# First products of an FFN: eight column tiles instead of four, the new four in seven block products

## The chip, the cores and the metric

The kernel runs on one core of a Trainium2 chip. The metric is the device time of one execution in microseconds (us). TensorE (PE) multiplies matrices into PSUM; VectorE (DVE) and ScalarE (ACT) work on tiles in SBUF and PSUM; GpSimd (POOL) does a little; SyncE (SP) issues the transfers from memory.

## The reference

Two layers (DEPTH = 2) of a post-norm encoder on 256 tokens of width 1024, all in float32:

```
for l in range(DEPTH):
    x = layer_norm(ALPHA * x + 0.5 * swiglu(x, ffn1_w_in[l], ffn1_w_out[l]), ...)
    x = layer_norm(ALPHA * x + hybrid_mixer(x, ...), ...)
    x = layer_norm(ALPHA * x + 0.5 * swiglu(x, ffn2_w_in[l], ffn2_w_out[l]), ...)

def swiglu(x, w_in, w_out):
    h = x @ w_in                               # 1024 -> 2 * 2816
    gate, up = h[..., :D_FF], h[..., D_FF:]
    return (silu(gate) * up) @ w_out           # 2816 -> 1024
```

The mixer (differential attention beside windowed attention) isn't touched by the change. There are four FFNs, two in each layer: (l, n) = (0, 0), (0, 2), (1, 0), (1, 2).

## The kernel before, in words

**Two halves of every number.** Most products are made in the type fp32r. Each operand is split in a high half (a cast to fp32r on ScalarE) and a low half (the value less the high half, on VectorE), and a product is made of three matmuls: high by high, high by low, low by high. `Weights._make` loads a row of weights (128 x 1024, 512 KB, issued on SP) into a `raw` buffer (there are 5), casts it to `wh` (L118) and subtracts it to `wl` (L119); there are 9 buffers of each. The window LOOK keeps at most nine of these slots ahead of use. The two instructions of a split have a priority lowered by LATER.

**An FFN.** The 2816 hidden columns are 22 column tiles of 128, each with a gate and an up half, and the 1024 inputs are 8 row tiles. Tokens come in two halves t of 128.

- `first`: the first four column tiles (NB = 4) with the tokens stationary: for each t and each of the 8 weight rows, three matmuls for gate and three for up, 512 columns wide. Then SiLU and a product (`gvb`, L390), and `first_t` transposes the result on TensorE (L397) and splits it into `gs` (L401, L402). In the first FFN both t run over the rows in one pass, and the DMA of the inputs has only begun; in the others t = 0 has its own pass, in which x of t = 1 is transposed by `to_xt`, and t = 1 has a second pass over the same 8 rows, which frees their slots.
- `col`: the other 18 column tiles with the weights stationary: for gate and up each 8 wide matmuls (both halves of all 256 tokens, 512 columns, L419) and 8 narrow ones (the weights' low half by the tokens' high half, 256 columns, L424). One tile alone comes first (column tile 4), then `first_t` of t = 1, then another one alone (column tile 5), then couples of two. With `flip` the narrow ones come first. After each tile comes an epilogue: a copy (L434), an addition (L435), SiLU (L436), the product (L438) and the split (L441, L442).
- the out phase: the second product of the FFN. Ten of the 22 row tiles are taken in five pairs (`STR`, indices of pairs of column tiles), the others one by one (`step`). `pair` computes the product of a 2 x 2 block matrix (two token halves, two row tiles, two column halves) by seven block products instead of eight. For that `_make_pair` builds four sums of weight blocks on VectorE (L86 to L89), and splits three 1024-wide tiles and one 512-wide (L72, L73); a pair takes 3 `raw` buffers, 4 slots of `wh` and `wl`, and one `tmp` tile. `sums` builds four sums of blocks of the activations (L457 to L462).
- then the tail of single steps, and the layer norm.

**What sets the order.** TensorE's order is the program's. The other engines' instructions are ordered by a scheduler at compile time by priority; each engine then runs its own list in order. Tiles of one tag share their buffers: `g` has 11, `tmp` 7, `x` 5, PSUM 8 (the pool `ps`, a bank each). The rotary table is computed on VectorE in the first FFN behind the first couple of column tiles.

Of the kernel before, what the change touches and what calls it, by code (L numbers as in the profile page):

```python
# [9 lines left out]
F32 = mybir.dt.float32  # L10
F32R = mybir.dt.float32r
# [8 lines left out]
P = 128  # L20
SEQ = 256
# [33 lines left out]
0; P sq 1 1; V 1; O 0 2; T sq 1; O 0 2; B 0 0; S s 1; B 0 1; Y 1; W 0 0; W 0 1; S s 1; O 1 1; O 0 1; O 1 1; O 0  # L55
3; B 1 0; B 1 1; W 1 0; W 1 1; O 1 2; Z; O 1 4
"""


class Weights:  # L60
# [15 lines left out]
    def _make_pair(self, i):  # L76


        nc, dv = self.nc, self.nc.vector
        r0, r1, ta = (self.pool.tile([P, 1024], F32, tag="raw", name=f"raw{i}{c}", bufs=5) for c in "abt")  # L80
        for r, src in zip((r0, r1), self.srcs[i][1:]):
            nc.sync.dma_start(r, src)
        t4 = self.tmp.tile([P, 512], F32, tag="tmp", name=f"t4_{i}")
        a, b = slice(0, 512), slice(512, 1024)
        with self.tc.high_priority(-LATER):
            dv.tensor_tensor(ta[:, a], r0[:, b], r0[:, a], ALU.subtract)  # L86
            dv.tensor_tensor(ta[:, b], r0[:, b], r1[:, b], ALU.add)
# [11 lines left out]
    def _make(self, i):  # L99
        nc = self.nc  # L100
        if self.srcs[i][0] == "S":
            return self._make_pair(i)
        raw = self.pool.tile([P, 1024], F32, tag="raw", name=f"raw{i}", bufs=5)
        wh = self.pool.tile([P, 1024], F32R, tag="wh", name=f"wh{i}", bufs=9)
        wl = self.pool.tile([P, 1024], F32R, tag="wl", name=f"wl{i}", bufs=9)

        n = 512 if i < 3 else 1024
        src = self.srcs[i]

        rows = src if isinstance(src, tuple) else (src,)  # L110
        for c in range(0, 1024, n):
            s = slice(c, c + n)
            for q, r in enumerate(rows):
                h = P // len(rows)

                (nc.sync if i or c else nc.scalar).dma_start(raw[q * h : (q + 1) * h, s], r[:, s])
            with self.tc.high_priority(0 if i < 3 else -LATER):
                nc.scalar.copy(wh[:, s], raw[:, s])  # L118
                nc.vector.tensor_tensor(wl[:, s], raw[:, s], wh[:, s].bitcast(F32), ALU.subtract)  # L119
        self.made.append((wh, wl))  # L120
# [15 lines left out]
def encoder_kernel(  # L136
# [44 lines left out]
    def out_rows(w):  # L181
        row = lambda k: w[k * P : (k + 1) * P, :]
        rows = [row(k) if u == "o" else ("S", row(2 * k), row(2 * k + 1)) for u, k in plan]
        return rows + [row(k) for k in tail]

    srcs = []
    for l in range(DEPTH):
        srcs += [f1_b[l, k] for k in range(KT)]
        srcs += [f1_in[l, j, s] for j in range(JT - NB) for s in range(2)]
        srcs += out_rows(f1_out[l])  # L190
        for c in range(3):
            srcs += [m_in[l, c, q] for q in range(4)]
# [6 lines left out]
        srcs += [f2_b[l, k] for k in range(KT)]  # L199
        srcs += [f2_in[l, j, s] for j in range(JT - NB) for s in range(2)]  # L200
        srcs += out_rows(f2_out[l])
    W = Weights(tc, wp, tp, srcs)
    wi = 0
# [113 lines left out]
        nc.sync.dma_start(bt, ln_b[l, n].partition_broadcast(P))  # L317
        return gt, bt

    def to_xt(src, t, nm, hs=(0, 1), gain=None):  # L320

        with tc.high_priority():
            for h in hs:
                tr = ps.tile([P, 4, P], F32, tag="b", name=f"tr_{nm}{t}{h}")
                for i in range(4):
                    c = (4 * h + i) * P
                    nc.tensor.transpose(tr[:, i, :], src[:, c : c + P], ident)
                dh = xx[:, 4 * h : 4 * h + 4, 0, t, :]
                dl = xx[:, 4 * h : 4 * h + 4, 1, t, :]
                if gain is None:  # L330
                    nc.scalar.copy(dh, tr)
                    dv.tensor_tensor(dl, tr, dh.bitcast(F32), ALU.subtract)
                else:
                    nc.scalar.mul(dh, tr, gain)
                    dv.scalar_tensor_tensor(dl, tr, gain, dh.bitcast(F32), ALU.mult, ALU.subtract)
# [25 lines left out]
    def ffn(l, n, last=False):  # L361
        nonlocal wi
        nm = f"{l}{n}"
        gs = [gp.tile([P, 2, 2, SEQ], F32R, tag="g", name=f"g_{nm}_{q}") for q in range(JT // 2)]

        def first(ts, mid=None):

# [23 lines left out]
                out.append(gv)  # L391
            return out

        def first_t(gv, t):
            tr = ps.tile([P, 4, P], F32, tag="b", name=f"trg_{nm}{t}")
            for i in range(4):
                nc.tensor.transpose(tr[:, i, :], gv[:, i * P : (i + 1) * P], ident)  # L397
            for q in range(2):
                a = slice(t * P, (t + 1) * P)
                dh = gs[q][:, :, 0, a]  # L400
                nc.scalar.copy(dh, tr[:, 2 * q : 2 * q + 2, :])  # L401
                dv.tensor_tensor(gs[q][:, :, 1, a], tr[:, 2 * q : 2 * q + 2, :], dh.bitcast(F32), ALU.subtract)  # L402

        def col(*js, flip=False):

            nonlocal wi
            ts = []
            for j in js:

                hs = [ps.tile([P, 2, SEQ], F32, tag="b", name=f"h{'gu'[s]}_{nm}_{j}") for s in range(2)]  # L410
                tl = tp.tile([P, 2, SEQ], F32, tag="tl", name=f"tl_{nm}_{j}", bufs=2)
                ws = [W.get(wi), W.get(wi + 1)]
                wi += 2
                ts.append((j, hs, tl, ws))

            def wide(hs, ws, s):
                for k in range(KT):

                    mm(hs[s], ws[s][0][:, k * P : (k + 1) * P], xx[:, k], start=(k == 0 and not flip),  # L419
                       stop=(k == KT - 1 and flip), skip_group_check=flip)  # L420

            def narrow(hs, ws, s):
                for k in range(KT):
                    mm(hs[s][:, 1, :], ws[s][1][:, k * P : (k + 1) * P], xx[:, k, 0], start=(k == 0 and flip),  # L424
                       stop=(k == KT - 1 and not flip), skip_group_check=flip)

            one, two = (narrow, wide) if flip else (wide, narrow)
            for j, hs, tl, ws in ts:
                for s in range(2):
                    one(hs, ws, s)  # L430
            for j, hs, tl, ws in ts:
                for s in range(2):
                    two(hs, ws, s)
                    nc.scalar.copy(tl[:, s], hs[s][:, 1, :])  # L434
                    dv.tensor_tensor(tl[:, s], hs[s][:, 0, :], tl[:, s], ALU.add)  # L435
# [3 lines left out]
                q, jj = divmod(j, 2)  # L439
                n = P if q in STR and jj == 0 else SEQ  # L440
                nc.scalar.copy(gs[q][:, jj, 0, 0:n], gv[:, 0:n])  # L441
                dv.tensor_tensor(gs[q][:, jj, 1, 0:n], gv[:, 0:n], gs[q][:, jj, 0, 0:n].bitcast(F32), ALU.subtract)  # L442
                if q in STR and jj:
                    sums(q, ts[0][2][:, 1], gv)

        sm = {}

# [18 lines left out]
        if first_x:  # L466
            g0, g1 = first((0, 1))
        else:
            (g0,) = first((0,), lambda: to_xt(x[1], 1, f"x{nm}"))
            (g1,) = first((1,))  # L470
        wi += KT
        if not first_x:
# [89 lines left out]
        todo += [(i, [c]) for c in fin for i in range(TAIL - SPLIT, TAIL)]  # L562
        for n_, (i, cs) in enumerate(todo):
            if n_ == len(todo) - TCUT and not last:
                to_xt(x[0], 0, f"y{nm}")
# [18 lines left out]
    def mixer(l):  # L584
# [263 lines left out]
        for tok in ORDER.split(";"):  # L848
# [37 lines left out]
            elif op == "X":  # L886
                to_xt(x[1], 1, f"m{l}")
            elif op == "Z":
                to_xt(x[0], 0, f"z{l}")
            elif op == "S":  # L890
                do_s(*ar)
            elif op == "A":
# [89 lines left out]
```

## Time and profile before

| | |
|---|---|
| three runs, us | 931.63, 931.92, 932.51 (median 931.92) |
| the profiled execution | 931.88 us, span 930.1 us, granted clock 0.997 |
| busy us: PE, DVE, ACT | 922.0, 789.5, 569.1 |
| transfers | 176.29 MB, mean 190 GB/s |

The span is from the first to the last recorded instruction. In the profile "PE" is the matmuls, "PEld" the loading of stationary operands, "xN" the number of instructions. In lists of instructions in order of time the columns are start (us), duration (us), engine, line, operation, output and inputs, shapes, and in brackets how long the engine sat idle before it and what ended that. The stages by TensorE in order: first FFN 4.8 to 186 us, mixer to 283, second FFN to 464, third FFN to 645, mixer to 743, fourth FFN to the end.

### The profile page before, as it was taken

Reading aid. Unit: us, or ns where it says so; the run is one execution under the profiler, and the core shown is the slowest. Engines: PE = TensorE matmul, PEld = TensorE weight load, DVE = VectorE, ACT = ScalarE, POOL = GpSimd, SP = SyncE. Lnnn points to the kernel's source line nnn. Section 1 sums busy time; section 2 is a strip of 40 time slices with the busy share of each in tenths; the row PEclk is TensorE's granted clock in tenths of the full one; section 3 lists DMA queues with packets and bytes.
Section 4 is the critical chain, followed back from the end, with each engine's and each line's share of the span. In section 5 each row is a group of like instructions: output and inputs, shape, how many; then the busy total and the mean of one; then the engine's idle time right before and its main releaser. Section 6 shows DMA issues by size and latency. Waiting matters only on the chain.

```text
span 930.1 us, 13767 instructions
## 1 busy us (share of the span) xinstructions
PE 922.0 (99%) x4970; PEld 788.2 (85%) x4970; DVE 789.5 (85%) x1344; ACT 569.1 (61%) x970; POOL 17.0 (2%) x27
## 2 busy tenths in 40 slices
PE   9999999999999999999999999999999999999996
PEld 7888888888888888888888888888888889888885
DVE  7898899998987678899986888999988976888896
ACT  5768656546865666656546666663478656666650
POOL 0000000000000000000000000000000000000000
PEclk9999999999999999999999999999999999999998
DMA  9986546675426755547675665575844365665551
GB/s 315 310 271 202 159 145 218 226 248 152 125 90 206 245 181 181 161 154 218 224 254 191 187 194 162 158 254 175 275 112 137 107 228 188 193 190 159 159 180 46
DMA packets 51379, 176.29 MB, mean 190 GB/s; under 512 B 6512, under 2 KB 8304, under 8 KB 51312
## 3 DMA queue, kind: packets, MB, share of 16 engines
q1 hardware_dynamic: 51024, 175.03, 58.7%
q8 instruction: 39, 0.64, 0.3%
q10 hardware_dynamic: 288, 0.39, 0.1%
q14 instruction: 28, 0.23, 0.1%
HBM read 174.35 MB, written 1.05 MB: 189 GB/s over the span
## 4 chain that ended last, share of the span: by engine, by line
PE 99%; DVE 1%; issue 0%; DVEq 0%
PE hg L419 14%; PE hu L419 14%; PE acc L503 14%; PE hb L381 9%; PE hu L424 7%; PE hg L424 7%; PE pp L527 6%; PE ao L840 5%; PE acc L527 4%; PE os L776 1%; PE pj_sq L619 1%; PE pj_sq L617 1%; PE pj_dv L617 1%; PE pj_sq L618 1%; PE pj_dq L617 1%; PE pj_dv L619 1%
## 5 line engine op out<-in xcount | busy, mean ns | idle before, releaser
L119 DVE TENSOR_TENSOR wl<-raw,wh 128x1024 fp32r<-128x1024 f32 (+1 forms) x279 | 336.1, 1210 | 73.7 <-PE hg L424 28.8
L118 ACT CAST wh<-raw 128x1024 fp32r<-128x1024 f32 (+1 forms) x279 | 290.6, 1047 | 117.4 <-PE acc L503 29.3
L419 PE MATMUL hg<-xx,wh 128*128 128x512 f32 x576 | 143.2, 391 | 0.0
L419 PE MATMUL hu<-xx,wh 128*128 128x512 f32 x576 | 142.3, 389 | 0.0
L419 PEld LDWEIGHTS hu<-xx,wh 128*128 128x128 f32 x576 | 108.1, 188 | 22.5
L419 PEld LDWEIGHTS hg<-xx,wh 128*128 128x128 f32 x576 | 106.6, 188 | 21.2
L503 PE MATMUL acc<-wh,g 128*128 128x512 f32 (+1 forms) x390 | 109.0, 387 | 0.0
L503 PEld LDWEIGHTS acc<-wh,g 128*128 128x128 f32 x390 | 72.9, 188 | 14.7
L424 PE MATMUL hg<-xx,wl 128*128 128x256 f32 x576 | 81.0, 283 | 0.0
L424 PE MATMUL hu<-xx,wl 128*128 128x256 f32 x576 | 80.9, 283 | 0.0
L424 PEld LDWEIGHTS hg<-xx,wl 128*128 128x128 f32 x576 | 75.4, 192 | 1.6
L424 PEld LDWEIGHTS hu<-xx,wl 128*128 128x128 f32 x576 | 74.3, 192 | 0.0
L381 PE MATMUL hb<-wh,xx 128*128 128x512 f32 x256 | 70.3, 395 | 0.0
L503 PE MATMUL acc<-wl,g 128*128 128x512 f32 (+1 forms) x195 | 61.6, 386 | 0.0
L381 PEld LDWEIGHTS hb<-wh,xx 128*128 128x128 f32 x256 | 48.3, 190 | 10.5 <-ACT wh L118 0.6
L434 ACT COPY tl<-hg 128x256 f32<-128x256 f32 x72 | 26.8, 372 | 32.0 <-PE hg L419 28.1
L503 PEld LDWEIGHTS acc<-wl,g 128*128 128x128 f32 x195 | 36.6, 188 | 7.3
L434 ACT COPY tl<-hu 128x256 f32<-128x256 f32 x72 | 26.8, 372 | 20.2 <-PE hu L424 17.1
L381 PE MATMUL hb<-wl,xx 128*128 128x512 f32 x128 | 38.9, 391 | 0.0
L840 PE MATMUL ao<-wh,xx 128*128 128x512 f32 x128 | 37.0, 398 | 0.0
L441 ACT CAST g<-tl 128x128 fp32r<-128x128 f32 (+1 forms) x72 | 27.1, 376 | 15.9 <-DVE tl L438 14.0
L436 ACT ACTIVATE tl<-tl 128x256 f32<-128x256 f32 x72 | 30.2, 419 | 6.5 <-DVE tl L435 5.6
(972 smaller groups left out, 1477.4 us busy)
## 6 DMA issues: line engine op xcount, KB each, us to landing
raw<-in_f_in_dram SPq DMA_DIRECT2D x144, 512.0 KB, 4.4
raw<-in_f_out_dram SPq DMA_DIRECT2D x48, 512.0 KB, 4.1
raw<-in_m_in_dram SPq DMA_DIRECT2D x36, 512.0 KB, 4.7
raw<-in_f_b_dram SPq DMA_DIRECT2D x29, 512.0 KB, 4.3
raw<-in_m_out_dram SPq DMA_DIRECT2D x8, 512.0 KB, 4.7
raw<-in_m_out_dram SPq DMA_DIRECT2D x16, 256.0 KB, 4.4
lng<-in_ln_g_dram SPq DMA_DIRECT2D x6, 512.0 KB, 4.9
lnb<-in_ln_b_dram SPq DMA_DIRECT2D x6, 512.0 KB, 6.0
```

The lines of the kernel that those rows point to most:

```text
L118: nc.scalar.copy(wh[:, s], raw[:, s])
L119: nc.vector.tensor_tensor(wl[:, s], raw[:, s], wh[:, s].bitcast(F32), ALU.subtract)
L381: mm(hb[s], xx[:, k, g, t, :], ww[:, 512 * s : 512 * s + 512], start=(k == 0 and e == 0), stop=(k == KT - 1 and e == 2))
L419: mm(hs[s], ws[s][0][:, k * P : (k + 1) * P], xx[:, k], start=(k == 0 and not flip), stop=(k == KT - 1 and flip), skip_group_check=flip)
L424: mm(hs[s][:, 1, :], ws[s][1][:, k * P : (k + 1) * P], xx[:, k, 0], start=(k == 0 and flip), stop=(k == KT - 1 and not flip), skip_group_c ...
L434: nc.scalar.copy(tl[:, s], hs[s][:, 1, :])
L436: nc.scalar.activation(tl[:, 0], tl[:, 0], AF.Silu)
L441: nc.scalar.copy(gs[q][:, jj, 0, 0:n], gv[:, 0:n])
L503: mm(a, g, ww[:, s], start=(k == ka and e == 0), stop=(k == kb and e == 2))
L527: mm(o, g, ww, start=(own and first and e == 0), stop=(own and final and e == 2))
L617: mm(o, xx[:, k, 0, t, :], wh[:, s], start=(k == 0), stop=False)
L840: mm(acc[t][h], xx[:, k, g, t, :], ww[:, s], start=(k == 0 and e == 0), stop=(k == KT - 1 and e == 2))
```

## The change

The tokens-stationary part now takes eight column tiles (NB = 8): the first four (NF = 4) as before, the next four in `group`. There the product of the tokens (two halves t by two row tiles of a pair k) and the weights (two row tiles by gate and up, 512 columns each) is made by seven block products of three matmuls each, for four pairs of row tiles, accumulated in seven PSUM banks: 84 matmuls of 512 columns. `_make_pair` makes the weights' sums as in the out phase, for four pairs in a row. `x_sums` makes four sums of blocks of x and their splits, from an unsplit copy of the transposed x (`xkeep`), which `to_xt` now stores by one more ScalarE copy per half, at a priority lowered by KEEP; in the first FFN it comes by two DMAs of 512 KB, issued on SP. The group's results are put together by nine VectorE instructions and three on ScalarE; two more calls of `first_t` transpose them after column tile 9.

The order in an FFN is now: `first` (rows 0 to 7), `first_t` (in the first FFN later), `x_sums`, column tile 8, `first_t`, `group`, column tile 9, `first_t` twice, the couples 10 and 11 to 20 and 21. The weights are fetched in that order: 8 rows, 2 rows of column tile 8, 4 pairs, the other columns' rows. The weights of the eight tiles lie together in memory, so that the 8 rows and the pairs' rows are read in runs of 2 KB per partition instead of 4 KB. STR goes from (3, 4, 5, 6, 7) to (5, 6, 7, 8, 9). The `gs` tiles are allocated one by one when first written.

```diff
-NB = 4
+NF = 4
+KEEP = 20
+NB = 8
-STR = (3, 4, 5, 6, 7)
+STR = (5, 6, 7, 8, 9)
...
+    def in_rows(b, w):
+        blk = lambda g, k: b[k].rearrange("p (s g c) -> p g s c", s=2, g=NB // NF)[:, g]
+        cols = [w[j, s] for j in range(JT - NB) for s in range(2)]
+        return [blk(0, k) for k in range(KT)] + cols[:2] + [("S", blk(1, 2 * k), blk(1, 2 * k + 1)) for k in range(KT // 2)] + cols[2:]
...
-        srcs += [f1_b[l, k] for k in range(KT)]
-        srcs += [f1_in[l, j, s] for j in range(JT - NB) for s in range(2)]
+        srcs += in_rows(f1_b[l], f1_in[l])
...
                     nc.scalar.copy(dh, tr)
                     dv.tensor_tensor(dl, tr, dh.bitcast(F32), ALU.subtract)
+                    if keep:
+                        with tc.high_priority(-KEEP):
+                            nc.scalar.copy(xkeep[t][:, 4 * h : 4 * h + 4, :], tr)
...
+        def split(src, nm_):
+            s = gp.tile([P, 2, 4, P], F32R, tag="g", name=f"sx_{nm}_{nm_}")
+            nc.scalar.copy(s[:, 0], src)
+            dv.tensor_tensor(s[:, 1], src, s[:, 0].bitcast(F32), ALU.subtract)
+            return s
+
+        def x_sums():
+            v = [xkeep[t].rearrange("p (k e) c -> p k e c", e=2) for t in range(2)]
+            a11, a12, a21, a22 = v[0][:, :, 0], v[0][:, :, 1], v[1][:, :, 0], v[1][:, :, 1]
...
+            dv.tensor_tensor(s1, a21, a22, ALU.subtract)
+            dv.tensor_tensor(s2, a11, s1, ALU.subtract)
+            dv.tensor_tensor(s3, a21, a11, ALU.subtract)
+            dv.tensor_tensor(s4, a12, s2, ALU.subtract)
...
+        def group(xs):
+            b = {c: ps.tile([P, 512], F32, tag="b", name=f"pg_{nm}_{c}") for c in range(1, 8)}
+            for k in range(KT // 2):
+                b11, b21, b22, t4, t1, t2, t3 = W.get(wi)
+                wi += 1
...
+                what = {1: (blk(0, 0), b11), 2: (blk(1, 0), b21), 3: (s4, b22), 4: (blk(1, 1), t4),
+                        5: (s1, t1), 6: (s2, t2), 7: (s3, t3)}
+                for c in (2, 3, 5, 7, 1, 6, 4) if k < KT // 2 - 1 else (1, 2, 6, 7, 5, 3, 4):
+                    (ah, al), (bh, bl) = what[c]
+                    for e, (a_, w_) in enumerate(((ah, bh), (ah, bl), (al, bh))):
+                        mm(b[c], a_, w_, start=(k == 0 and e == 0), stop=(k == KT // 2 - 1 and e == 2))
+            f = lambda c: tp.tile([P, 512], F32, tag="tmp", name=f"gr_{nm}_{c}")
+            add = lambda o, p, v: dv.tensor_tensor(o, p, v, ALU.add)
...
+            nc.scalar.copy(v, b[1])
+            add(g0, b[2], v)
+            nc.scalar.activation(g0, g0, AF.Silu)
+            add(v, b[6], v)
+            add(w, b[7], v)
+            add(v, b[5], v)
+            add(u1, b[5], w)
+            add(v, b[3], v)
+            dv.tensor_tensor(v, g0, v, ALU.mult)
+            add(w, b[4], w)
+            nc.scalar.activation(w, w, AF.Silu)
+            dv.tensor_tensor(w, w, u1, ALU.mult)
+            return v, w
...
+        if first_x:
+            for t in range(2):
+                xkeep[t] = gp.tile([P, KT, P], F32, tag="g", name=f"xf_{nm}{t}")
+                nc.sync.dma_start(xkeep[t], x_tr[:, t])
+        else:
             first_t(g0, 0)
+        xs = x_sums()
         col(NB)
         if first_x:
             first_t(g0, 0)
         first_t(g1, 1)
+        ga, gb_ = group(xs)
         for j in (NB + 1, *range(NB + 2, JT, 2)):
             col(*((j,) if j == NB + 1 else (j, j + 1)), flip=(j % 4 == 0 or j == NB + 1))
+            if j == NB + 1:
+                first_t(ga, 0, NF // 2)
+                first_t(gb_, 1, NF // 2)
```

More of the change, by code (lines that the diff above doesn't have):

```diff
@@ L57, with _cols @@
 """
+def _cols(t, like):
+    return t if len(like.shape) == 2 else t.rearrange("p (s c) -> p s c", s=like.shape[1])
 class Weights:
@@ L198, in encoder_kernel @@
                  for n in range(KT // 2)]
[L199 to L200 removed]
+        srcs += in_rows(f2_b[l], f2_in[l])
         srcs += out_rows(f2_out[l])
@@ L363, in ffn, with g_tiles @@
         nm = f"{l}{n}"
-        gs = [gp.tile([P, 2, 2, SEQ], F32R, tag="g", name=f"g_{nm}_{q}") for q in range(JT // 2)]
+        gs = {}
+        def g_tiles(*qs):
+            for q in qs:
+                gs[q] = gp.tile([P, 2, 2, SEQ], F32R, tag="g", name=f"g_{nm}_{q}")
         def first(ts, mid=None):
@@ L392, in first, with first_t @@
             return out
-        def first_t(gv, t):
-            tr = ps.tile([P, 4, P], F32, tag="b", name=f"trg_{nm}{t}")
+        def first_t(gv, t, q0=0):
+            if not t:
+                g_tiles(q0, q0 + 1)
+            tr = ps.tile([P, 4, P], F32, tag="b", name=f"trg_{nm}{t}{q0}")
             for i in range(4):
@@ L468, in ffn @@
         else:
-            (g0,) = first((0,), lambda: to_xt(x[1], 1, f"x{nm}"))
+            (g0,) = first((0,), lambda: to_xt(x[1], 1, f"x{nm}", keep=True))
             (g1,) = first((1,))
         wi += KT
-        if not first_x:
+        if first_x:
+            for t in range(2):
+                xkeep[t] = gp.tile([P, KT, P], F32, tag="g", name=f"xf_{nm}{t}")
+                nc.sync.dma_start(xkeep[t], x_tr[:, t])
+        else:
             first_t(g0, 0)
+        xs = x_sums()
         col(NB)
```

34 lines of the change are left out of this document (27 added, 7 removed).

## The prediction

> **What bounds the kernel now.** I read the page's busy shares first, then the chain that ended last, then stretches of the span by engine, and last the instructions in order of time around the edit.
>
> ```profile
> span 930.1 us, 13767 instructions
> PE 922.0 (99%) x4970; PEld 788.2 (85%) x4970; DVE 789.5 (85%) x1344; ACT 569.1 (61%) x970; POOL 17.0 (2%) x27
> ...
> PE 99%; DVE 1%; issue 0%; DVEq 0%
> ```
>
> TensorE is busy 922.0 of 930.1 us and carries 99% of the chain: today nothing else ends last. VectorE follows with 789.5, so it has about 140 us to spare in the whole program. What matters is where that spare time lies:
>
> ```profile
> 0.00:24.00 24.00, 23.23 (x90) 17.25 (x91) 17.07 (x24) 13.64 (x16) 1.63 (x11) 1.00 0.90 314
> 27.60:33.10 5.50, 5.50 (x34) 4.88 (x33) 5.50 (x6) 3.86 (x6) 0.00 (x0) 1.00 0.97 316
> 27.60:165.80 138.20, 138.20 (x750) 120.44 (x749) 122.00 (x226) 95.98 (x154) 0.00 (x0) 1.00 0.67 216
> 283.30:306.40 23.10, 23.10 (x110) 19.23 (x109) 17.12 (x22) 11.78 (x13) 1.00 (x1) 1.00 0.67 220
> 312.00:406.80 94.80, 94.80 (x550) 84.10 (x548) 75.35 (x139) 60.42 (x109) 0.00 (x0) 1.00 0.55 169
> 406.80:444.20 37.40, 37.40 (x167) 30.97 (x166) 34.35 (x39) 23.32 (x27) 0.00 (x0) 1.00 0.67 210
> ```
>
> A row gives the stretch and its length, then busy us of PE, PEld, DVE (VectorE), ACT (ScalarE) and POOL, the granted clock, the DMA share and GB/s. In an FFN's column tiles it has 19.5 us of 94.8 free, spread out, while the out phase with its block products keeps it at 34.35 of 37.40. Around the place of the edit in the very first FFN (27.6 to 33.1) it is full already.
>
> **TensorE's part of the change.** Four column tiles leave the old scheme, seven block products for four pairs of row tiles come in.
>
> ```profile
> 54.48 1.84 PE hg L419 x8
> 76.69 1.84 PE hg L419 x8
> 135.18 2.72 PE pp L527 x12
> 305.81 0.60 PE L397 MATMUL trg<-ident,gvb 128*128 128x128 f32 x4
> 306.17 2.09 PE L419 MATMUL hg<-xx,wh 128*128 128x512 f32 x8
> ```
>
> Two flips apart, four column tiles take 76.69 - 54.48 = 22.21 us. Twelve block-product matmuls take 2.72, 0.227 each, and the group has 4 x 7 x 3 = 84: 19.04, or 4.76 a pair. Four transposes take 306.17 - 305.81 = 0.36; eight more cost 0.72. TensorE saves 22.21 - 19.04 - 0.72 = 2.45 us an FFN, **9.8 us in four**, if it never waits.
>
> **VectorE's part.** What counts is the distance between starts, since an instruction's reported end overlaps the next start:
>
> ```profile
> 425.88 1.22 DVE L73 TENSOR_TENSOR wl139t<-raw139t,wh139t 128x1024 fp32r<-128x1024 f32 x1
> 427.02 1.22 DVE L73 TENSOR_TENSOR wl139a<-raw139a,wh139a 128x1024 fp32r<-128x1024 f32 x1
> 428.16 0.69 DVE L86 TENSOR_TENSOR raw140t<-raw140a 128x512 f32<-128x512 f32 x1
> 428.76 0.69 DVE L73 TENSOR_TENSOR wl139f<-t,wh139f 128x512 fp32r<-128x512 f32 x1
> 429.36 0.69 DVE L87 TENSOR_TENSOR raw140t<-raw140a,raw140b 128x512 f32<-128x512 f32 x1
> ...
> 349.60 0.42 DVE L435 TENSOR_TENSOR tl<-hg,tl 128x256 f32<-128x256 f32 x1
> 349.93 0.42 DVE L435 TENSOR_TENSOR tl<-hu,tl 128x256 f32<-128x256 f32 x1
> ```
>
> 1024 columns: 1.14; 512: 0.60; 256: 0.33. Removed per FFN: eight row splits (9.1) and four column epilogues of four 256-wide instructions (5.3), 14.4 in all. Added: four weight pairs, each four block sums, three 1024 splits and one 512 split (5 x 0.60 + 3 x 1.14 = 6.42), 25.7; x_sums, four sums and four splits, 4.8; the group's epilogue, nine instructions, 5.4; four 256 splits, 1.3. Together 37.2. Net **+22.8 an FFN**, 91 in four: 789.5 becomes about 881 of a TensorE-only span of some 920. It fits on average. It does not fit locally: a pair costs VectorE 6.42 and TensorE 4.76, and four stand in a row.
>
> [...] If each instruction held the engine for its reported 1.22 or 0.69, a pair would cost 7.1 and the sum below would end near 957. The starts 0.60 apart at durations of 0.69 disagree, so the pitch stands and that end gets no chance below.
>
> **Where the group waits.** In the last pair the products run b11 first, so it needs nearly the whole pair made (all but the 512 split t4). I compare when TensorE is due at pair 4 with when VectorE can have made it, counting its work from when it is next free. Second FFN:
>
> ```profile
> 289.36 1.41 DVE L355 SCALAR_TENSOR_TENSOR x<-x,rs,lnb 128x512 f32<-128x512 f32 x2
> 292.56 1.29 DVE L332 TENSOR_TENSOR xx<-tr_x,xx 128x512 fp32r<-128x512 f32 x2 [1.79 <-ACT xx L331]
> 295.53 0.69 DVE L390 TENSOR_TENSOR gvb<-sgb,hb 128x512 f32<-128x512 f32 x1 [1.68 <-ACT sgb L388]
> 297.58 8.03 DVE L119 TENSOR_TENSOR wl<-raw,wh 128x1024 fp32r<-128x1024 f32 x6 [1.35 <-ACT wh L118]
> ```
>
> Layer norm ends at 290.8. The three gaps behind it (1.79, 1.68, 1.35) and everything from 297.6 are open to new work; the wait at 297.58 is for slots of the row weights, which block sums and x_sums don't need. Due: column tile 306.17 + 5.55 (a quarter of 22.21), 0.36 of transposes, three pairs of 4.76: 326.4. Needed before it: three pairs 19.3, the fourth without t4 5.8, x_sums 4.8, one column row 1.1, xx 1.2, two gvb 1.2, first_t 1.3, the column's epilogue 1.3: 36.0. Without a gap that ends at 326.8, and at the out phase's 92% (34.35 of 37.40) at 329.9. TensorE waits 0.4 to 3.5; I take 2.0. Net -0.45. The last FFN repeats this stage 459.4 later: -0.45.
>
> Third FFN:
>
> ```profile
> 471.07 2.35 DVE L119 TENSOR_TENSOR wl<-raw,wh 128x1024 fp32r<-128x1024 f32 x2
> 473.44 1.29 DVE L332 TENSOR_TENSOR xx<-tr_x,xx 128x512 fp32r<-128x512 f32 x2
> ...
> 487.30 1.85 PE hg L419 x8
> ...
> 306.42 1.85 PE hg L419 x8
> ```
>
> TensorE is 180.9 later than in the second (487.30 against 306.42), so due at 507.3; VectorE is free only at 473.4, ready at 509.4 to 512.5. Wait 2.1 to 5.2, taken 3.7: net +1.25.
>
> First FFN. The weights come at the DMA's pace: by 24.0 us 24 x 314 GB/s = 7.5 MB have landed, of which x and the eight rows are 5.2, so four more 0.5 MB blocks: two column rows and pair 1. VectorE has caught up by then:
>
> ```profile
> 18.53 6.35 DVE L119 TENSOR_TENSOR wl<-raw,wh 128x1024 fp32r<-128x1024 f32 x5
> 26.23 1.23 DVE L119 TENSOR_TENSOR wl<-raw,wh 128x1024 fp32r<-128x1024 f32 x1 [1.35 <-PE hb L381]
> 32.95 1.04 PE L397 MATMUL trg<-ident,gvb 128*128 128x128 f32 x8
> 33.74 1.20 PE L424 MATMUL hg<-xx,wl 128*128 128x256 f32 x8
> ```
>
> From 24.0: pair 1 without its first sum 5.8, pairs 2 and 3 12.8, the fourth 5.8, x_sums 4.8 (its 1 MB of x, queued behind pair 1 on SP, lands some 3 us later and the pair's own work fills that), gvb 1.2, first_t 1.3, the epilogue 1.3: 33.0, so 57.0, or 59.9 at 92%. The group starts at 33.74, pair 4 is due at 48.0. **Wait 9.0 to 11.9, taken 10.0**: net +7.55. Behind the group stands the rotary table, which needs VectorE where there is no spare time now:
>
> ```profile
> L275 DVE SCALAR_TENSOR_TENSOR rt<-rt 128x64 f32<-128x64 f32 x14 | 3.1, 220 | 0.0
> ```
>
> With as many smaller ones beside these 3.1 us, an estimate of 6 us; tiles 12 and 13 start with their low halves and would wait for them 0 to 4. I take 2.
>
> Costed at nothing: ScalarE (at 61%; it makes one copy for each split of VectorE's, so its extra is below 91 us and its spare 361; if it fell behind, the splits behind each copy would wait in order); seven of eight PSUM banks, since column tile 8's two are read out within some 2 us and the product that takes the last comes 2 us into the group (0 to 1 us); low halves for column tile 9, made while pair 4 runs; the keep copies; the moved STR, whose same sums come four tiles later and are still ready before the out phase. After the group VectorE has per two tiles 4 x 1.14 + 8 x 0.33 and the sums of a couple, under 2 (an estimate from the widths above), 9 of 11.1 us, so the lead it lost is regained in the six following couples.
>
> **Sum**: 7.55 + 2 - 0.45 + 1.25 - 0.45 = +9.9 on the profiled execution's 931.88 (span 930.1 and 1.8 around it; the median of the runs is 931.92): **941.8**. With all waits at their low ends (9.0, 0, 0.4, 2.1, 0.4) it is +2.1, 934.0; at their high ends (11.9, 4, 3.5, 5.2, 3.5) +18.3, 950.2. That is the likeliest case's own range.
>
> **Rivals.**
> - VectorE keeps up and TensorE stays the bound: -9.8, 922.1. For it: the waits of FFNs two to four are small sums of large numbers, and earlier spare time (17.12 of 23.10 busy) could take more. Against: the first FFN's 9 us rests on landing times. It decides if pair 1 is made in the first FFN before 20 us and the others start ahead of 290. [...]
> - Half and half: the first wait is about 5 and the others vanish; gains and waits cancel, 930 to 934.
> - The lost lead isn't regained. If VectorE runs no stretch better than 92%, the first FFN's 122.0 + 22.8 us take 157 instead of 138, and the second's 17.12 + 75.35 + 34.35 + 22.8 take 163 where its three stretches have 155: +19 and three times +7, 972. I count half of it, 952. For it: the out phase is at that share; against: columns have slack after the group.
> - First-product rows now come in runs of 2 KB, not 4. Against 409 GB/s with mostly long runs stood 270 with short ones:
>
> ```profile
> 4.00:8.00 4.00, 4.00 (x13) 2.85 (x12) 3.21 (x7) 1.60 (x3) 0.00 (x0) 1.00 0.94 270
> 12.00:16.00 4.00, 4.00 (x19) 3.34 (x18) 3.04 (x4) 2.64 (x3) 0.00 (x0) 1.00 1.04 409
> ```
>
>   At 270, five rows (2.6 MB) and pair 1 (1 MB) land 4.6 us later and the first FFN's chain with them: 946. Against: the early stretch also has the smaller x blocks. [...]
>
> **Chances.** Forecast 0.55, keeps up 0.17, cancels 0.10, lead lost 0.10, short runs 0.08. Faster by over 0.2% (1.9 us, about what a measurement can tell here) 0.20, within 0.10, slower 0.70. Range: 926 (the better half of the keeps-up case left out) to 953.
>
> **What would show it.** Right: gaps of PE before the block products of pairs 2 to 4, released by VectorE's splits wl of those pairs, some 10 us in the first FFN and 0 to 5 in the others; VectorE at 95% or more there; its total near 880; TensorE's busy time about 10 us less. Wrong: no PE gap in the first group, or waits that end on a DMA, on PSUM banks or on x_sums' own copies on ScalarE; or a PE pitch in the group other than 0.227.

## The result and the profile after

The changed kernel takes 954.62 us (median; 953.34 to 955.44) against 931.91: a ratio of 1.0243, 95% interval 1.0231 to 1.0256. It is slower by 22.7 us. The forecast was +9.9, and the time lies 1.6 us above the range's upper end of 953. Ratios here and below are against the kernel before, with the 95% interval in brackets. One of the ten executions of the kernel with single rows in all four FFNs, below, took 3301.84 us where the nine others took 933.45 to 933.88, and is left out of its ratio.

The page of the changed kernel, in the order in which that of the kernel before was read (span, busy shares, the chain by engine):

```profile
span 953.6 us, 13658 instructions
PE 925.7 (97%) x4826; PEld 778.4 (82%) x4826; DVE 870.6 (91%) x1460; ACT 596.3 (63%) x993; POOL 17.0 (2%) x27
...
PE 81%; DVE 13%; DMA 3%; ACT 1%; issue 1%; SPq 0%; DVEq 0%; ACTq 0%
```

TensorE issues 144 matmuls fewer, and yet its busy time is 925.7 where it was 922.0: a matmul of 512 columns is recorded with 0.63 us where the granted clock was 0.50 and with about 0.50 alone beside a wait (below), instead of 0.39 in the groups' undisturbed stretches. VectorE went from 789.5 to 870.6, and it now stands in the chain with 13%.

The share of the loss that each FFN has can be read from the first matmul of each out phase. The timeline of the changed kernel, and of the kernel before:

```profile
141.03 0.62 PE L596 MATMUL acc<-wh,g 128*128 128x512 f32 x2
422.70 0.61 PE L596 MATMUL acc<-wh,g 128*128 128x512 f32 x2
607.26 0.62 PE L596 MATMUL acc<-wh,g 128*128 128x512 f32 x2
889.90 0.62 PE L596 MATMUL acc<-wh,g 128*128 128x512 f32 x2
```

```profile
128.22 0.62 PE L503 MATMUL acc<-wh,g 128*128 128x512 f32 x2
406.67 0.62 PE L503 MATMUL acc<-wh,g 128*128 128x512 f32 x2
587.55 0.62 PE L503 MATMUL acc<-wh,g 128*128 128x512 f32 x2
866.03 0.62 PE L503 MATMUL acc<-wh,g 128*128 128x512 f32 x2
```

The lag is 12.8, 16.0, 19.7 and 23.9 us, so the four FFNs cost 12.8, 3.2, 3.7 and 4.2 us.

Inside an FFN there are two stops. The first is in the group. In the second FFN the group runs from its first block product to the low half that follows it:

```profile
325.06 0.48 PE L512 MATMUL pg<-wh93b,xx 128*128 128x512 f32 x1
...
341.27 0.49 PE L512 MATMUL pg<-wh96a,xx 128*128 128x512 f32 x1 [1.13 <-ACT wh96a L78]
342.94 0.50 PE L512 MATMUL pg<-wl96a,xx 128*128 128x512 f32 x1 [1.17 <-DVE wl96a L79]
...
347.62 0.52 PE L449 MATMUL hg<-xx,wl 128*128 128x256 f32 x3
```

It takes 22.56 us where 84 matmuls at 0.227 are 19.04. Of the excess of 3.52, 0.64 stands in pair 1 (5.40 us from start to start, in place of 4.76) and 2.88 at pair 4 (row 96). A bracket gives TensorE's idle time and its releaser; the two hold 2.30, and the rest is that a lone matmul is recorded with 0.49 where the next one otherwise starts after 0.227. The releasers are the cast and the split of one block of pair 4's weights. The cast had itself waited for VectorE: it starts at 340.18, after 0.74 us idle, when VectorE has made the block `raw96a` (second row below). VectorE at that time, without a gap:

```profile
338.19 1.22 DVE L79 TENSOR_TENSOR wl96b<-raw96b,wh96b 128x1024 fp32r<-128x1024 f32 x1
339.33 0.68 DVE L94 TENSOR_TENSOR raw96a<-raw96b,raw96t 128x512 f32<-128x512 f32 x1
339.93 1.22 DVE L79 TENSOR_TENSOR wl96t<-raw96t,wh96t 128x1024 fp32r<-128x1024 f32 x1
341.06 0.68 DVE L95 TENSOR_TENSOR t<-raw96b,raw96a 128x512 f32<-128x512 f32 x1
341.67 1.22 DVE L79 TENSOR_TENSOR wl96a<-raw96a,wh96a 128x1024 fp32r<-128x1024 f32 x1
```

The second stop comes behind column tile 9, where the group's results are transposed:

```profile
354.06 0.66 PE L422 MATMUL trg<-ident,gr_v 128*128 128x128 f32 x4 [0.71 <-DVE gr_v L524]
355.56 0.66 PE L422 MATMUL trg<-ident,gr_w 128*128 128x128 f32 x4 [0.84 <-DVE gr_w L527]
355.98 1.39 PE L444 MATMUL hg<-xx,wh 128*128 128x512 f32 x5
```

The eight transposes were to take 0.72. From the end of column tile 9 (347.62 + 5.58 = 353.20) to the next matmul it is 2.78, so 2.06 us are lost. VectorE is in the middle of the group's epilogue here, with splits of the next rows (L127) between its sums:

```profile
347.47 0.68 DVE L514 TENSOR_TENSOR gr_v<-pg,gr_v 128x512 f32<-128x512 f32 x1
348.07 1.21 DVE L127 TENSOR_TENSOR wl<-raw,wh 128x1024 fp32r<-128x1024 f32 x1
349.20 0.68 DVE L514 TENSOR_TENSOR gr_w<-pg,gr_v 128x512 f32<-128x512 f32 x1
...
354.82 0.69 DVE L527 TENSOR_TENSOR gr_w<-gr_w,gr_u 128x512 f32<-128x512 f32 x1 [0.47 <-ACT gr_w L526]
```

In the third FFN it is the same, with 0.89 us of VectorE's own wait for the cast of a row among it. In the first and the fourth FFN (1.57 us lost in each) TensorE waits for gr_w alone, 1.28 us by the bracket, and there VectorE is not busy. It stands idle before the last product of the epilogue, 1.92 and 1.47 us. In the first FFN:

```profile
72.19 0.37 ACT L459 COPY tl<-hu 128x256 f32<-128x256 f32 x1 [0.50 <-PE hu L444]
72.47 0.63 ACT L526 ACTIVATE gr_w<-gr_w 128x512 f32<-128x512 f32 x1
73.13 0.69 DVE L527 TENSOR_TENSOR gr_w<-gr_w,gr_u 128x512 f32<-128x512 f32 x1 [1.92 <-ACT gr_w L526]
```

VectorE had made the input of this SiLU by 70.27 (the sum starts at 69.59 and takes 0.68). But in ScalarE's own order the SiLU stands behind a copy of column tile 9 (L459), which can only come when TensorE has finished that tile. So the wait is one of order on ScalarE there, and not of VectorE's work.

The third loss is in no bracket. After the long wait of the first FFN, stretches of the span (PE, PEld, DVE, ACT and POOL busy, then the granted clock, DMA share and GB/s) and the rows within them:

```profile
56.00:60.00 4.00, 1.41 (x3) 0.99 (x4) 4.00 (x6) 3.02 (x4) 0.00 (x0) 0.75 0.51 160
60.00:64.00 4.00, 4.00 (x11) 3.04 (x11) 4.00 (x5) 3.57 (x5) 0.00 (x0) 0.50 1.00 331
```

```profile
57.44 0.51 PE L512 MATMUL pg<-wh13a,xx 128*128 128x512 f32 x1 [2.66 <-ACT wh13a L78]
59.10 0.80 PE L512 MATMUL pg<-wl13a,xx 128*128 128x512 f32 x1 [1.16 <-DVE wl13a L79]
...
60.12 0.63 PE L512 MATMUL pg<-wh13b,xx 128*128 128x512 f32 x1
60.55 0.63 PE L512 MATMUL pg<-wl13b,xx 128*128 128x512 f32 x1
```

From 60 to 64 us the granted clock is 0.50, and the matmuls start 0.43 us apart in place of 0.227: TensorE is "busy" 4.00 of 4.00 us with 11 matmuls, where 21 stand in the same stretch of warm_late14 (below). The same pitch stands in pair 1 of this group, from 38.11 to 40.67, behind a single idle time of 1.92 us; the granted clock from 38.0 to 40.6 is 0.50 too.

Counted from the rows of all four groups (32.64, 22.56, 22.56 and 24.05 us), the excess over 19.04 is 25.65 us: 5.25 of it are matmuls about 0.43 apart (4.05 in the first FFN, of which 1.2 in pair 1, and 1.20 in the fourth), the other 20.4 are waits with the lone matmuls around them. The transposes lose 1.57, 2.06, 2.57 and 1.57 beyond their 0.72, 7.8 in all. With the 9.8 saved: 20.4 + 5.25 + 7.8 - 9.8 = +23.6, and the span grew by 23.5.

### The profile page after: what moved, and what is told of

Same layout as the page of the kernel before. It is cut to its first block, busy times and chain, and to the rows that moved or that the text cites. A ratio compares the mean times of both kernels' runs of the same rounds, so it can differ in the third digit from the quotient of the medians.

```text
span 953.6 us, 13658 instructions
## 1 busy us (share of the span) xinstructions
PE 925.7 (97%) x4826; PEld 778.4 (82%) x4826; DVE 870.6 (91%) x1460; ACT 596.3 (63%) x993; POOL 17.0 (2%) x27
## 4 chain that ended last, share of the span: by engine, by line
PE 81%; DVE 13%; DMA 3%; ACT 1%; issue 1%; SPq 0%; DVEq 0%; ACTq 0%
PE acc L596 13%; PE hg L444 10%; PE hu L444 10%; PE pp L620 6%; PE hb L404 5%; PE hu L449 5%; PE hg L449 5%; PE ao L933 5%; PE acc L620 4%; PE pg L512 2%; DMA raw<-in_f_in_dram 1%; DVE sx L476 1%; DMA raw<-in_f_b_dram 1%; DVE t L95 1%; PE os L869 1%
## 5 line engine op out<-in xcount | busy, mean ns | idle before, releaser
L126 ACT CAST wh<-raw 128x1024 fp32r<-128x1024 f32 (+1 forms) x247 | 256.2, 1045 | 115.9 <-DMA raw<-in_f_in_dram 28.9
L127 DVE TENSOR_TENSOR wl<-raw,wh 128x1024 fp32r<-128x1024 f32 (+1 forms) x247 | 294.5, 1205 | 29.6 <-ACT wh L126 18.0
L444 PE MATMUL hg<-xx,wh 128*128 128x512 f32 x448 | 111.9, 392 | 0.0
L444 PE MATMUL hu<-xx,wh 128*128 128x512 f32 x448 | 110.7, 389 | 0.0
L444 PEld LDWEIGHTS hu<-xx,wh 128*128 128x128 f32 x448 | 84.1, 188 | 17.6
L444 PEld LDWEIGHTS hg<-xx,wh 128*128 128x128 f32 x448 | 82.6, 188 | 16.2
L449 PE MATMUL hg<-xx,wl 128*128 128x256 f32 x448 | 62.7, 283 | 0.0
L459 ACT COPY tl<-hu 128x256 f32<-128x256 f32 x56 | 20.9, 373 | 12.7 <-PE hu L449 9.7
L404 PEld LDWEIGHTS hb<-wl,xx 128*128 128x128 f32 x128 | 24.3, 190 | 5.1
L468 ACT CAST g<-tl 128x256 fp32r<-128x256 f32 (+1 forms) x56 | 20.7, 370 | 11.8 <-DVE tl L463 10.6
L933 PEld LDWEIGHTS ao<-wh,xx 128*128 128x128 f32 x128 | 23.3, 188 | 5.4 <-issue 0.8
```

Source lines behind the costliest of these rows:

```text
L404: mm(hb[s], xx[:, k, g, t, :], ww[:, 512 * s : 512 * s + 512], start=(k == 0 and e == 0), stop=(k == KT - 1 and e == 2))
L933: mm(acc[t][h], xx[:, k, g, t, :], ww[:, s], start=(k == 0 and e == 0), stop=(k == KT - 1 and e == 2))
```

## The experiments

The theory to test: VectorE's added work makes TensorE wait twice in an FFN (pair 4, transposes), and an idle TensorE then pays a third time in clock. The rivals: rows or buffers that come late, the layout in 2 KB runs, the moved STR. No run puts the SiLU of gr_w earlier in ScalarE's order; its part in the transposes' wait is read from the trace alone.

**The transposes one couple later.**

```
-            if j == NB + 1:
+            if j == NB + 2:
                 first_t(ga, 0, NF // 2)
```

> The group's eight transposes come after the couple of column tiles 10 and 11 instead of after tile 9. Theory A (VectorE is late with the group's results, and TensorE waits for them at these transposes, 1.57 + 2.06 + 2.57 + 1.57 us in the four FFNs): that 7.8 us goes, 947, the waits before pair 4 stay at 10.8 and 3.4. Rival (VectorE has a backlog anyway, so the wait only moves to tiles 12 and 13, which start with low halves): 953 to 955.

Measured: 948.43 us, ratio 1.0174 (1.0156 to 1.0191), 6.2 us less than the change. The transposes in the second FFN, with no bracket left:

```profile
362.34 0.60 PE L422 MATMUL trg<-ident,gr_v 128*128 128x128 f32 x4
362.78 0.60 PE L422 MATMUL trg<-ident,gr_w 128*128 128x128 f32 x4
363.13 1.20 PE L449 MATMUL hg<-xx,wl 128*128 128x256 f32 x8
```

The time is near the theory's 947, and the rival's 953 is out. So the stop behind column tile 9 is shown, and what it cost: 6.2 us by the medians, 7.7 by the profiled spans (953.6 and 945.9), with the slow matmuls now in the third FFN's group (24.19) and no longer in the fourth's (22.76).

**The last pair in the order of the others**, so that b11 comes fifth in pair 4.

```
-for c in (2, 3, 5, 7, 1, 6, 4) if k < KT // 2 - 1 else (1, 2, 6, 7, 5, 3, 4):
+for c in (2, 3, 5, 7, 1, 6, 4):
```

> The last pair's products run in the order of the other pairs (2, 3, 5, 7, 1, 6, 4), so it can start when its first split is made instead of its third. Theory A (TensorE waits for the splits wl of pair 4 on VectorE, 10.8 and three times 3.4 us): the third split is due 2.7 us later, so 2 to 2.7 us go from each wait, 8 to 11 in all, but the group's results start some 3 us later and the wait at the transposes grows by 1 to 2 each: 947 to 953. Rival (the pair's weights land late): no change in the wait, 954 or more.

Measured: 961.29 us, ratio 1.0307 (1.0290 to 1.0324): slower, against the expectation. The groups came down as expected, to 27.01, 19.83, 20.06 and 19.85 us. But the transposes of the second FFN read:

```profile
353.78 0.66 PE L422 MATMUL trg<-ident,gr_v 128*128 128x128 f32 x4 [2.45 <-DVE gr_v L524]
356.68 1.12 PE L422 MATMUL trg<-ident,gr_w 128*128 128x128 f32 x4 [2.24 <-DVE gr_w L527]
357.45 2.76 PE L444 MATMUL hg<-xx,wh 128*128 128x512 f32 x6
```

The idle time there grew from 1.55 to 4.69 us: TensorE arrives earlier at a point that VectorE reaches no earlier, since its last split of pair 4 starts 17.7 us after the group in both kernels. The wait moved, and slow matmuls followed it: six matmuls of column tile 10 take 2.76, 0.43 apart, the pitch that went with a granted clock of 0.50 in the changed kernel; in the first, third and fourth FFN the eight behind the transposes take 3.64, 3.72 and 3.16, and the eight behind those 2.00, 2.00 and 1.98. Over the four FFNs the groups gave back 15.1 us, the stretches from the group's end to behind the transposes took 15.7 more, and the column tiles behind it, 66.7 us each in the changed kernel, are 67.8 to 68.4, together 5.5 longer. So the moved wait alone would have cost about what was won; most of the 6.7 us lost is these 5.5, with slow matmuls behind longer waits.

**Matmuls nobody reads, ahead of pair 4** (ten, on constant ones, into the eighth bank).

```
+            dmy = ps.tile([P, 512], F32, tag="b", name=f"dmy_{nm}")
...
+                if k == KT // 2 - 1:
+                    for _ in range(10):
+                        mm(dmy, one(1.0, [P, P], BF16), one(1.0, [P, 512], BF16), start=True, stop=True)
```

> Ten dummy matmuls (2.2 us) on a bank of their own stand in front of pair 4, inside the wait. If the slow clock behind the waits (0.50 granted at 60 to 64 us, 0.61 at 808 to 812) comes from TensorE's idling and costs what the slow matmuls of pair 4 show (2.8 us in the first FFN, 1.6 in the fourth), 950 and a granted clock of 1.0 there in the fourth FFN. If it doesn't come from idling, or its time is waited out elsewhere: 954 to 956.

Measured: 951.87 us, ratio 1.0210 (1.0195 to 1.0225), 2.75 us less than the change with 40 matmuls more, between the 950 of one expectation and the 954 of the other. In the fourth FFN the slow pitch is gone and the group takes 22.55 in place of 24.05; that one comparison could be luck, since late_t lost it there without any added matmul. In the first FFN the group takes 31.12 in place of 32.64, and eight slow matmuls remain at pair 4 (59.71 to 63.12): the ten end before the wait does, and 1.16 us of idle time still stand before its second product. Stretches of the changed kernel in the fourth FFN, then of this one:

```profile
808.00:812.00 4.00, 2.88 (x7) 2.30 (x8) 4.00 (x5) 3.94 (x5) 0.00 (x0) 0.61 0.89 303
```

```profile
808.00:812.00 4.00, 4.00 (x22) 3.41 (x21) 4.00 (x6) 3.60 (x6) 0.00 (x0) 1.00 1.01 360
```

**The pairs' block sums on GpSimd** in place of VectorE (`dv = nc.gpsimd` for the four sums of the group's pairs).

> The four block sums of each of the group's weight pairs are made on GpSimd instead of VectorE, whose pair falls from 6.42 to 4.0 us, below TensorE's 4.76. Theory A (VectorE's work is the bound of the group): the waits before pair 4 fall to 0 to 2 us in the first FFN and 0 in the others, the slow clock with them: 927 to 934, if GpSimd needs under 1.2 us a sum; with longer ones GpSimd is the bound and 940 to 970. Rival (landing of the weights, or ScalarE's casts): waits as before, 950 or more.

Measured: 999.4 us, ratio 1.0719 (1.0698 to 1.0741), far above the 970 of the theory; the rival's "950 or more" holds the number, but not by its waits, which were to stay as before. GpSimd and VectorE in the second FFN:

```profile
327.29 2.08 POOL L93 TENSOR_TENSOR raw94t<-raw94a 128x512 f32<-128x512 f32 x1 [11.88 <-issue]
329.33 2.27 POOL L94 TENSOR_TENSOR raw94t<-raw94a,raw94b 128x512 f32<-128x512 f32 x1
331.69 1.62 POOL L95 TENSOR_TENSOR raw94a<-raw94b,raw94t 128x512 f32<-128x512 f32 x1
```

```profile
330.38 1.78 DVE L79 TENSOR_TENSOR wl93f<-t,wh93f 128x512 fp32r<-128x512 f32 x1
332.08 2.31 DVE L79 TENSOR_TENSOR wl94b<-raw94b,wh94b 128x1024 fp32r<-128x1024 f32 x1
334.31 1.21 DVE L79 TENSOR_TENSOR wl94t<-raw94t,wh94t 128x1024 fp32r<-128x1024 f32 x1
```

A sum takes GpSimd 1.62 to 2.27 us in these rows where VectorE took 0.68 in the changed kernel, and of VectorE's own splits one of 512 columns takes 1.78 in place of 0.68 and one of 1024 takes 2.31 in place of 1.22 while GpSimd runs. The move costs VectorE more than it takes off: with 64 instructions fewer it is busy 883.8 us in place of 870.6. No wait is left before pair 4 in the second to fourth FFN; TensorE now stands 6.2 us in each of them before the first product of pair 1 that reads the split sums of x, which VectorE makes too late. So the run shows what the move costs, and decides nothing between the theory and the rival.

**VectorE's share of the block sums of x left out.**

```
-            dv.tensor_tensor(s1, a21, a22, ALU.subtract)
...
+            for i, a in enumerate((v[1][:, :, 0], v[0][:, :, 0], v[1][:, :, 1], v[0][:, :, 1])):
+                s = gp.tile([P, 2, 4, P], F32R, tag="g", name=f"sx_{nm}_{i}")
+                nc.scalar.copy(s[:, 0], a)
+                nc.scalar.copy(s[:, 1], a)
...
```

> The changed kernel with VectorE's share of the token blocks' sums left out: the four tiles sx are filled by two ScalarE copies each of blocks of the kept activations, so the products of the group are of wrong blocks (sums and low halves of x are left out), with the same matmuls. VectorE has 8 instructions fewer, 0.60 us apart each: 4.8 us an FFN. Theory (pair 4 is late because VectorE has no time left): the three waits of 3.4 us end, the first falls from 10.8 to about 6, half of the 4.5 us of slow clock goes with them: 954.6 - 10.1 - 4.8 - 2.3 = about 937, the range 934 to 941. Rival (pair 4 is late because its buffers come free late, or its rows do): the waits stay and the time is 952 to 955.

Measured: 936.89 us, ratio 1.0055 (1.0040 to 1.0070), as the theory had it and not the rival. The second FFN's group, first and following row:

```profile
319.91 0.48 PE L504 MATMUL pg<-wh93b,xx 128*128 128x512 f32 x1
...
339.08 0.40 PE L449 MATMUL hg<-xx,wl 128*128 128x256 f32 x2
```

19.17 us for the same 84 matmuls with the same weights by the same transfers; the third and fourth groups take 19.17 too. So pair 4's rows and buffers are there in time in these three, and what was missing is 4.8 us of VectorE. ScalarE makes eight copies here where it made four casts, so it wasn't the limit either. The first group takes 27.51: pair 4 still waits there for its cast and its split (2.06 and 1.16 us idle), and 12 slow matmuls follow.

**Tokens stationary alone, in all four FFNs**: eight single rows in place of four pairs, no block products and no sums, with the same 2 KB runs and STR.

```
+PLAIN = lambda l, n: True
...
+            [blk(1, k) for k in range(KT)] if plain else [("S", blk(1, 2 * k), blk(1, 2 * k + 1)) for k in range(KT // 2)]
...
-        ga, gb_ = group(xs)
+            ga, gb_ = first((0, 1))
+            wi += KT
```

> One part of the change alone, in all four FFNs: column tiles 4 to 7 with tokens stationary from the same rows in 2 KB runs and with the same STR, but as eight single rows times two token tiles (96 matmuls of 512 columns), with no block products, no pairs and no sums on VectorE. Theory (the loss is VectorE's sums alone): TensorE has 96 x 0.227 = 21.8 us and 0.72 of transposes in place of 22.21, so +0.3 an FFN, and up to 1 us more where the transposes wait for the last product on VectorE: 931.9 + 1 to + 5, so 933 to 937. Rival (the 2 KB runs or the moved STR cost something by themselves): 938 to 946.

Measured: 933.77 us, ratio 1.0019 (1.0010 to 1.0029). The bulk of the loss is in the pairs and sums; layout, STR, the added transposes and the 96 matmuls in place of the column tiles are together worth 1.9 us (0.9 to 2.7), and the rival of short runs, with its 938 or more, is out.

**Order and later transposes together.** The edits of the first two experiments.

> The changed kernel with the last pair's products in the order of the other pairs and the group's transposes one couple of column tiles later. Theory (two separate waits: pair 4 in the group, the group's sums at the transposes): the group's waits fall to what the order alone left, 8.0 + 0.8 + 1.0 + 0.8 = 10.6 us in four with the clock in them, the transposes wait for nothing, TensorE has 9.8 us less: 931.9 + 0.8 = about 933, up to 936 with slow clock elsewhere. Rival (VectorE owes the work, and the wait only moves again, to the couple's banks or to the next weights): 940 to 948.

Measured: 935.94 us, ratio 1.0043 (1.0026 to 1.0060). The order alone lost 6.7 us and the later transposes alone won 6.2; together they win 18.7. With the transposes out of the way, the wait that the order had only moved is gone, and so are the slow matmuls behind it. The first FFN's group still takes 26.99.

**The same, with single rows in the first FFN.**

```
+PLAIN = lambda l, n: l == 0 and n == 0
```

> As order_late, and in the first FFN alone the second four column tiles run as eight single rows with tokens stationary (no pairs, no sums there). Theory: the first FFN comes to 21.8 + 0.72 - 22.21 = +0.3 us against the kernel before, the other three to 19.04 + 0.9 of wait + 0.72 - 22.21 = -1.55 each: 931.9 + 0.3 - 4.7 = about 927.5, the range 926 to 930. Rival (the wait of VectorE moves to a later place): 932 to 942.

Measured: 928.17 us, ratio 0.9961 (0.9946 to 0.9976): 0.4% faster than the kernel before. The second FFN's group takes 19.82, the third's 19.88, the fourth's 19.85.

**More unread matmuls, and the transposes later** (40 in the first FFN, 14 in the others).

> The changed kernel with the group's transposes one couple later (as late_t) and matmuls of ones into the eighth bank, read by nobody, ahead of pair 4 (40 in the first FFN, 14 in the others), so that TensorE does not stand idle before pair 4. The wait for VectorE stays. Theory (waits and slow clock after an idle TensorE are separate terms): only the waits of 10.8 + 3 x 3.4 = 20.9 us stay against the 9.8 saved, 931.9 + 11.1 = 943, up to 945 where the added matmuls reach past the wait. Rival (the clock is not set by the idle time): the time of late_t, 948.

Measured: 948.62 us, ratio 1.0181 (1.0167 to 1.0195), the rival's number. The trace shows why it can't decide for the rival:

```profile
62.28 1.04 PE L506 MATMUL dmy<-const-bfloat16-1.0 128*128 128x512 bf16 x4
62.96 0.58 PE L516 MATMUL pg<-wh13a,xx 128*128 128x512 f32 x1
```

In the first FFN the added matmuls ran until 62.96, past the 57.44 and 59.10 at which pair 4 was made in the changed kernel. I had sized them for 10.8 us of wait at pair 4; but of the first group's excess 6.5 us stand in pairs 1 to 3. The forty were too many there.

**Fourteen in every FFN.**

> As warm_late with 14 matmuls of ones in every FFN. In warm_late the first FFN's 40 ended at 62.96 us, and the changed kernel began pair 4's second product at 59.10: they reached 3.9 us past the wait, since some 6 of the 10.8 us of wait lie in pairs 1 to 3. Theory (clock a term of its own): the group of the first FFN comes to about 29.8 us (31.6 in late_t, 33.8 in warm_late), the other three stay at 22.8, the sum at 98.2 against 101.1 in late_t: 948.4 - 2.9 = 945.5, the range 944.5 to 946.5. Rival (the clock does not depend on the idle time): 948 to 949.

Measured: 944.46 us, ratio 1.0138 (1.0119 to 1.0157), 4.0 less than late_t (3.3 by the profiled spans, 942.6 and 945.9), at the lower edge of the theory's range. The stretch after the first FFN's wait:

```profile
60.00:64.00 4.00, 4.00 (x21) 3.35 (x20) 4.00 (x5) 3.54 (x6) 0.00 (x0) 1.00 0.98 368
```

Clock 1.00 where it was 0.50, and 21 matmuls in place of 11. The groups take 30.14, 22.81, 22.81 and 23.02: the first and the third are shorter than in late_t (31.57 and 24.19), the wait for VectorE stands. Together they take 98.8 in place of 101.1, so 2.3 us are the experiment's; another 0.9 lies ahead of the first group, where the two kernels are the same, and is chance. Behind the wait at pair 4 slow matmuls followed in four of the eight groups of the changed kernel and late_t, and in none of the eight with 14 or 40 unread matmuls in that wait. The clock is a cost of its own here, by these 2.3 us.

**The sums of x earlier**, on top of first_plain: emitted in the first pass, as soon as the second token tile is transposed.

```
+            def mid():
+                to_xt(x[1], 1, f"x{nm}", keep=not PLAIN(l, n))
+                xs.extend(x_sums())
...
-            xs = x_sums()
```

> As first_plain, with the sums of the token blocks emitted in the first pass over the first four column tiles, as soon as the second token tile is transposed, where VectorE stood idle for 2.0 us before the product of the first token tile. Theory (pair 4 waits for VectorE's work, whatever it is): those 2 us are used, and the waits of 0.8 to 1.0 us left in three FFNs end: 928.2 - 2.7 = about 925.5, the range 924.5 to 927. Rival (what is left of the waits is ScalarE's casts or the rows' buffers): 927.5 to 929.5; and if the sums there delay the splits of the first rows, over 929.5.

Measured: 926.19 us, ratio 0.9942 (0.9929 to 0.9954), the fastest of all. The second FFN's group:

```profile
312.91 0.48 PE L515 MATMUL pg<-wh97b,xx 128*128 128x512 f32 x1
...
332.08 0.40 PE L452 MATMUL hg<-xx,wl 128*128 128x256 f32 x2
```

19.17 again, as where the sums were left out; the fourth's is 19.17, the third's 20.03. Its rest of a wait is VectorE's too: the fourth pair takes 5.64 in place of 4.76, and its first low half, for one, is read at 506.67, 0.08 us after VectorE's split of it ends.

## Why the prediction was wrong, step by step

- **Right: the direction, the cause of the group's wait and TensorE's saving.** Pair 4 waits for VectorE's block sums and splits, in all four FFNs; leaving 4.8 us of VectorE's work out ends three of those waits. The 0.227 a block product held where neither waits nor slow matmuls stood in a group (19.17 us for 84 in nox and sums_early).
- **"Where the group waits", about right in sum.** Taken were 10.0, 2.0, 3.7 and 2.0, 17.7 together; measured 9.6, 3.5, 3.5 and 3.8, 20.4. The second came out at its high end, 3.5, which was worked out at 92%, and the fourth just above it: I had counted VectorE's gap before its first gvb as open to new work; in the changed kernel it is still there, since x_sums stand behind both gvb in VectorE's order (first row below). sums_early put them into it, and what the order had left of the wait, in pair 1 before the last of the split sums, went (19.82 to 19.17). In the first FFN the size was right and the place was not: 4.3 us before pair 4, the rest in pairs 1 to 3, from the split sums of x on (second row). A wait that ends on their copy on ScalarE was named as a sign of being wrong; that copy had itself waited 0.58 us for VectorE's sum.

```profile
309.48 0.69 DVE L413 TENSOR_TENSOR gvb<-sgb,hb 128x512 f32<-128x512 f32 x1 [1.97 <-ACT sgb L411]
...
36.63 0.50 PE L512 MATMUL pg<-wh10b,sx 128*128 128x512 f32 x1 [1.92 <-ACT sx L475]
```

- **The step that failed: the eight transposes were priced at their own 0.72 us,** and a wait there at nothing, with no word on when gr_v and gr_w are made. They stand one column tile (5.58 us) behind the group, and the group's nine epilogue instructions, which I did count in VectorE's sum (5.4 us), run there in line with the splits of the next rows. In the first and fourth FFN it is ScalarE's order instead: the SiLU of gr_w comes behind the copy of column tile 9, and the prediction had judged ScalarE by its busy share. The term measured 7.8 us beyond its 0.72 an FFN, of the 12.8 missed; late_t gave 6.2 of it back.
- **The clock was in no term.** I worked with one pitch, and named another pitch only as a sign of error. Behind the waits that I forecast slow matmuls stood in two of the four groups: 5.25 us. With late transposes the four groups lost 2.3 us less when unread matmuls filled the wait (warm_late14 against late_t). So TensorE's busy time, which was to fall by about 10 us, rose by 3.7; VectorE's total came to 870.6 where 880 was expected.
- **The rotary table was over-priced**: 0 instead of 2.
- Together 2.7 on the waits, 7.8, 5.25 and -2: 13.7 above the forecast's +9.9, or 23.6 against 23.5 measured on the span.
- **The rivals.** "The lost lead isn't regained" did not come: after the transposes TensorE has no further gap before the out phase, so six couples do regain it. "2 KB runs" is at most a part of the 1.9 us of plain_all. "VectorE keeps up" is what first_plain and sums_early made of the change: with 845 us of VectorE work in place of 871 and the same block products in three FFNs.

What stays open: what an earlier SiLU of gr_w alone would have given, which wait brings a slow clock and which doesn't, and how the 1.9 us of plain_all divide between transposes, layout and STR (its expected +1.2 for TensorE's own work is most of it).

## What to carry to other kernels

A product that trades matmuls for sums on another engine has to be paid at its deadlines, not on average: list every point at which TensorE reads something that engine makes (here the split sums of x in pair 1, pair 4 and the transposes), and check each against that engine's program order. The order of every engine in between counts too: ScalarE's SiLU here came behind a copy that waits for TensorE. Fixing one of two such points in series can gain nothing, because TensorE then waits longer at the next; in order4 it lost 6.7 us, since matmuls 0.43 us apart followed the longer waits. Move the later consumer first. And a forecast TensorE wait should be priced with what the clock can take after it: here nothing behind the second and third FFN's 3.5 us, 1.2 behind the fourth's, 2.85 behind 4.3 at pair 4 of the first and 1.2 behind 1.9 in its pair 1, a quarter of all waits in sum.

## What the runs showed of the hardware

In the changed kernel the granted clock fell to 0.50 from 60 to 64 us, after the first FFN's wait, and matmuls of 512 columns then started 0.43 us apart instead of 0.227; in warm_late14, with fourteen unread matmuls in the wait, it was 1.00 in that stretch. The same wait of some 3.5 us was followed by slow matmuls in the fourth FFN (group 24.05) and by none in the second and third (22.56 each), and in late_t it was the third that had them (24.19). These waits are not one idle time: in the fourth FFN it is 1.12 and 1.16 us with a matmul between them. In the changed kernel's groups no unbroken idle time is longer than 2.66 us, and in pair 1 of the first FFN slow matmuls followed 1.92 us (1.87 there in late_t and 1.63 in order_late were followed by none). So these runs show no length of idle time that decides it.

In poolsum a sum of 512 columns took GpSimd 1.62 to 2.27 us in the three rows shown, where VectorE took 0.68 in the changed kernel; and while GpSimd ran, a VectorE split of 1024 columns took 2.31 beside 1.21 at the same line.
